# A decoder layer on one core: the DMAs that ScalarE issues are issued by GpSimd instead

## The chip, the cores and the metric

One Trainium2 chip, one of its cores. The metric is the device time of one execution in microseconds (us), as the median of the runs; lower is better. The engines are TensorE (PE; PEld is its weight load), VectorE (DVE), ScalarE (ACT), GpSimd (POOL) and SyncE (SP). SP, ACT and POOL issue DMAs in this kernel. A row that ends in q (ACTq) is an engine's sequencer, which issues or waits while the engine itself is idle.

## The reference, cut to what matters

```python
def reference(x, ...):                       # x: (1, 256, 2048), everything float32
    x = layer_norm(alpha * x + 0.5 * swiglu(x, ffn1...), ln1_g, ln1_b)      # d_ff 5632
    p = x @ w_in                             # 3072 attention columns, 3360 RWKV columns
    o_attn = diff_attn_group(p[..., :3072], ...)    # 8 heads, two softmaxes each, causal, ALiBi
    o_rwkv = rwkv7_group(p[..., 3072:], ...)        # 16 heads of 64, a recurrence over 256 steps
    mix = concatenate([o_attn, o_rwkv]) @ w_out
    x = layer_norm(alpha * x + mix, ln2_g, ln2_b)
    return layer_norm(alpha * x + 0.5 * swiglu(x, ffn2...), ln3_g, ln3_b)
```

The recurrence keeps a 64x64 state per head and updates it at every step by a decay, a rank-one correction and a rank-one addition.

## The kernel before, in words

Three stages follow one another: a feed-forward (FFN), the mixer, a second feed-forward. All large products go through one `Stream`: each weight tile (256 rows by 512 columns, `raw`) is loaded by SP (L125), split into a rounded part `wh` by ACT (L128) and a remainder `wl` by DVE (L129), and used by 12 matmuls (L105 to L107: two halves of the tokens, two row blocks, three products). Seven buffers of `wh` and `wl` let the split run ahead of the matmuls. "A stream step" below is one such tile, and "a stream matmul" one of its 12.

In the mixer the stream carries `w_in` and then `w_out`, and generators (`rwkv_group`, `rwkv_values`, `attn_heads`) put small pieces of background work between the steps. The RWKV heads come in two groups, r1 and r2, and the attention heads in two groups, a1 and a2; a group of attention runs two heads at a time, so a2 has a first and a second pass. `rwkv_group` replaces the recurrence by chunks: it computes products of the chunk's vectors into `Q` (L554 and L557), and needs the inverse of many 32x32 triangular matrices. For that inverse four DMAs rearrange pieces of `Q` into DRAM (`dU`, L566), one brings them back as `U` (L569), DVE runs 31 pairs of instructions (L577 and L579), copies the transposed result (L582), and two DMAs write `dY` and `dYT` (L583, L584), from which four fill `TT` (L591) and two fill `YT` (L595). The four `dU` and the four `TT` DMAs and the two of `YT` move runs of 32 numbers, 512 runs each. Then come products with `YT` (L602), `TT` (L613), transposes (L623), and four chunk steps c0 to c3 (L636, L644, L652, L669, L675), a norm over the heads (L689 to L709) and the gate (L720 to L724).

The output product is taken in three parts, and each part adds to `y`: first a1 and r1, then a2, and last r2.

```python
        for i, qs in enumerate(parts):       # parts = [(0, 2), (1,), (3,)]
            for q in qs:
                ready(q)                     # waits for the group's result and splits it (L78, L79)
            ...
            for n in range(4):
                stream.block(A["w_out"][0], n * NB, NB, ks, o_lhs, ...)
```

Part two needs a2 and has 8 stream steps, 96 matmuls; part three needs r2. Residual pieces `rc` are loaded at L252 (FFN) and L863 (mixer), and `x` is stored to `xs` at L190 between stages. GpSimd computes the powers for the norms (L180, L810), clears `TT` (L589), and loads tables and the norms' gains (L198 to L308).

The tile framework orders every engine's instructions when the program is built, by its own estimate of when each could start. On the chip every engine then takes its instructions in that fixed order. So a change of the issuing engine can reorder all the engines.

Of the kernel before, what the change touches and what calls it, by code (L numbers as in the profile page):

```python
# [20 lines left out]
NB = 512  # L21
# [16 lines left out]
def build(tc, A, out):  # L38
    nc = tc.nc
# [12 lines left out]
    def nm(s):  # L52
        uid[0] += 1
        return f"{s}_{uid[0]}"
# [8 lines left out]
    xs = [dp.tile([P, D], F32, tag=f"xs{t}", name=f"xs{t}") for t in range(2)]  # L63
# [5 lines left out]
    def transpose_split(src, tt, q, store, on_dve=False):  # L69
        tr = tr_bank[-1]()  # L70
        for j in range(4):
            T.transpose(tr[:, j, :], src[:, j * P:(j + 1) * P], ident)
        split(tr, store, tt, q, on_dve)
# [100 lines left out]
    def ln_tail(tt, y, st, gt, bt, last):  # L174
        mv = sp.tile([P, 2], F32, tag="mv", name=nm("mv"))
        V.bn_aggr(out=mv, in_=st)
        ve = sp.tile([P, 1], F32, tag="ve", name=nm("ve"))
        V.tensor_scalar(out=ve, in0=mv[:, 1:2], scalar1=LN_EPS, scalar2=None, op0=ALU.add)
        rs = sp.tile([P, 1], F32, tag="rs", name=nm("rs"))
        G.tensor_tensor(out=rs, in0=ve, in1=neghalf, op=ALU.pow)  # L180
        for q in range(4):
            c = slice(q * NB, (q + 1) * NB)
            yq = y[q]
            V.scalar_tensor_tensor(out=yq, in0=yq, scalar=mv[:, 0:1], in1=gt[:, c], op0=ALU.subtract, op1=ALU.mult)  # L184
            V.scalar_tensor_tensor(out=yq, in0=yq, scalar=rs, in1=bt[:, c], op0=ALU.mult, op1=ALU.add)  # L185
            if last:
                nc.sync.dma_start(out=out[tt * P:(tt + 1) * P, c], in_=yq)
            else:
                transpose_split(yq, tt, q, xT)
                nc.scalar.dma_start(out=xs[tt][:, c], in_=yq)  # L190

    def load_gb(pool, g, b, tg, tb, after=None):
        gt = (hp if tg == "J0" else pool).tile([P, D], F32, tag=tg, name=nm("lng"))
# [8 lines left out]
    def ffn(fp, wg, wu, wd, lg, lb, res, last, extra=None):  # L202
        y = [fp.tile([P, D], F32, tag=f"y{t}", name=nm("y")) for t in range(2)]
        st = [sp.tile([P, 4, 6], F32, tag=f"st{t}", name=nm("st"), bufs=1) for t in range(2)]
        gb = []
        j0 = 0
        for half, nj in enumerate((6, 5)):
            hT = {}
            sg = {}

            def gate_done(tt, acc):
                s = fp.tile([P, NB], F32, tag="sg", name=nm("sg"), bufs=2)
                SC.activation(out=s, in_=acc, func=AF.Silu)  # L213
                sg[tt] = s

            def up_done(tt, acc, j):
                h = fp.tile([P, NB], F32, tag="h", name=nm("h"), bufs=2)
                V.scalar_tensor_tensor(out=h, in0=sg[tt], scalar=0.5, in1=acc, op0=ALU.mult, op1=ALU.mult)  # L218
                tr = tr_bank[-1]()
                for i in range(4):  # L220
                    T.transpose(tr[:, i, :], h[:, i * P:(i + 1) * P], ident)  # L221
                if j < 3:
                    if tt == 0:
                        hT[j] = hp.tile([P, 4, 4, P], F32R, tag=f"J{j}", name=nm("hh"))
                    hi, lo = hT[j][:, 2 * tt], hT[j][:, 2 * tt + 1]
                else:
                    hl = hp.tile([P, 2, 4, P], F32R, tag=f"H{3 * tt + j - 3}", name=nm("hh"))
                    hi, lo = hl[:, 0], hl[:, 1]
                SC.copy(out=hi, in_=tr)  # L229
                V.tensor_tensor(out=lo, in0=tr, in1=hi.bitcast(F32), op=ALU.subtract)  # L230
                hT[(tt, j)] = (hi, lo)

            for j in range(nj):
                c0 = (j0 + j) * NB
                stream.block(wg, c0, NB, KX, x_lhs, gate_done)
                stream.block(wu, c0, NB, KX, x_lhs, lambda tt, acc, j=j: up_done(tt, acc, j))

            def h_lhs(tt, k, hT=hT):
                hi, lo = hT[(tt, k // 4)]
                return hi[:, k % 4, :], lo[:, k % 4, :]  # L240

            if half == 0 and extra is not None:
                extra(hT[(0, 0)][0][:, 0, 0:1].bitcast(F32))
            if half == 1:
                gb = load_gb(fp, lg, lb, "lng", "lnb", hT[(0, 0)][0][:, 0, 0:1].bitcast(F32))

            def down_done(tt, acc, n, half=half, hT=hT):
                c = slice(n * NB, (n + 1) * NB)
                if half == 0:
                    rc = fp.tile([P, NB], F32, tag="rc", name=nm("rc"), bufs=2)  # L250
                    G.tensor_copy(out=rc[:, 0:1], in_=hT[(0, 0)][0][:, 0, 0:1].bitcast(F32))
                    nc.scalar.dma_start(out=rc, in_=res[tt][:, c])  # L252
                    V.scalar_tensor_tensor(out=y[tt][:, c], in0=rc, scalar=ALPHA, in1=acc, op0=ALU.mult, op1=ALU.add)
                else:
                    V.tensor_tensor(out=y[tt][:, c], in0=y[tt][:, c], in1=acc, op=ALU.add)
                    V.bn_stats(out=st[tt][:, n, :], in_=y[tt][:, c])
                    if n == 3:
                        ln_tail(tt, [y[tt][:, i * NB:(i + 1) * NB] for i in range(4)], st[tt], gb[0], gb[1], last)

            for n in range(4):  # L260
                ks = [(j0 * 4 + k, k) for k in range(nj * 4)]
                stream.block(wd, n * NB, NB, ks, h_lhs, lambda tt, acc, n=n, f=down_done: f(tt, acc, n))
            j0 += nj
# [53 lines left out]
    def mix(mp, pq, C):  # L317
# [66 lines left out]
        res = {}  # L384
# [81 lines left out]
        def rwkv_group(g, st):  # L466
# [1 line left out]
            while prev is not None and "chain" not in prev:  # L468
                yield None
            wa = Qt[:, 0:NB]  # L470
            nc.scalar.dma_start(out=wa[0:64, :], in_=A["rwkv_w2"][0, :, g * NB:(g + 1) * NB])
            nc.scalar.dma_start(out=wa[64:128, :], in_=A["rwkv_a2"][0, :, g * NB:(g + 1) * NB])
            while "tw" not in lora:
                yield None
            lw = t4("lw")
# [84 lines left out]
            dU = dp.tile([64, 32, 32], F32, tag="dU", name=nm("dU"))  # L560
            dY = dp.tile([64, 32, 32], F32, tag="dY", name=nm("dY"))
            dYT = dp.tile([32, 32, 32], F32, tag="dYT", name=nm("dYT"))
            quad = [(d, e, slice(64 * e + 32 * d, 64 * e + 32 * d + 32), slice(32 * d, 32 * d + 32),
                     slice(32 * d + 16 * e, 32 * d + 16 * e + 16)) for d in range(2) for e in range(2)]
            for d, e, rr, cc, uu in quad:
                nc.scalar.dma_start(out=dU[uu].rearrange("u s t -> s u t"),  # L566
                                    in_=Q[rr, :, :, e, cc].rearrange("p a c t -> p (a c) t"))
            U = hp.tile([64, 32, 32], F32, tag=HT["T1"], name=nm("U"))
            nc.scalar.dma_start(out=U, in_=dU)  # L569
            Y = hp.tile([64, 32, 32], F32, tag=HT["T2"], name=nm("Y"))  # L570
            V.memset(Y, 0.0)
            V.memset(Y.rearrange("p a b -> p (a b)")[:, ::33], 1.0)
# [7 lines left out]
                if j % 2 == 0:  # L580
                    yield 1.0
            V.tensor_copy(out=U, in_=Y.rearrange("p a b -> p b a"))  # L582
            nc.scalar.dma_start(out=dY, in_=Y)  # L583
            nc.scalar.dma_start(out=dYT, in_=U[0:32])  # L584
            while "values" not in st:
                yield None
            SV = st["SV"]
            TT = hp.tile([P, 16, 64], F32, tag=HT["lw"], name=nm("TT"))
            G.memset(TT, 0.0)  # L589
            for d, e, rr, cc, uu in quad:  # L590
                nc.scalar.dma_start(out=TT[rr, :, cc], in_=dY[uu].rearrange("u s t -> s u t"))  # L591
            YT = hp.tile([P, 16, 32], F32, tag=HT["T1"], name=nm("YT"))
            PT = hp.tile([P, 16, 32], F32, tag=HT["T2"], name=nm("PT"))
            for e in range(2):
                nc.scalar.dma_start(out=YT[64 * e:64 * e + 32], in_=dYT[16 * e:16 * e + 16].rearrange("u s t -> s u t"))  # L595
            yield 0.6
            Qf = Q.rearrange("p a c e t -> p (a c) e t")
            ps = bank("sm", (P, 16, 32))
# [81 lines left out]

            st["chain"] = True
            g2a, g2b = Qt[:, 3072:3584], Qt[0:32, 3584:4096]
            nc.scalar.dma_start(out=g2a, in_=A["rwkv_g2"][0, 0:128, g * NB:(g + 1) * NB])
            nc.scalar.dma_start(out=g2b, in_=A["rwkv_g2"][0, 128:160, g * NB:(g + 1) * NB])
            for hf in range(2):
                h2 = slice(2 * hf, 2 * hf + 2)
                ps = bank("sm", (P, 2, S))
# [171 lines left out]
        def o_done(tt, acc, n, i):  # L859
            c = slice(n * NB, (n + 1) * NB)  # L860
            if i == 0:
                rc = mp.tile([P, NB], F32, tag="tm", name=nm("rc"), bufs=2)
                nc.scalar.dma_start(out=rc, in_=xs[tt][:, c])  # L863
                V.scalar_tensor_tensor(out=y[tt][n], in0=rc, scalar=ALPHA, in1=acc, op0=ALU.mult, op1=ALU.add)
            else:
                V.tensor_tensor(out=y[tt][n], in0=y[tt][n], in1=acc, op=ALU.add)  # L866
            if i == len(parts) - 1:
                V.bn_stats(out=st[tt][:, n, :], in_=y[tt][n])  # L868
                if n == 3:
                    ln_tail(tt, y[tt], st[tt], gb[0], gb[1], False)  # L870
# [79 lines left out]
```

## Time and profile before

| | |
|---|---|
| median of 3 runs | 2022.41 us (2021.51 to 2024.14) |
| the profiled execution: its time, its span | 2021.85 us, 2020.1 us |
| PE busy | 1976.9 us, 98% of the span, 9671 matmuls |
| DVE, ACT, POOL busy | 1149.0, 887.6, 33.9 us |
| DMA queue q10 (issued by ACT) | 17440 packets, 14.29 MB |
| DMA queue q0 (issued by POOL) | 1520 packets, 6.93 MB |
| granted TensorE clock | 0.989 of full speed on average |

PE is busy nearly all the time, so the page as a whole says little about what an off-path DMA is worth. The stretch that tells more is the mixer's end, from about 1148 us to 1234 us of the span: there the granted clock falls and PE waits.

### The profile page before, as it was taken

To read this page: it belongs to the slowest core of one execution; us is meant where nothing else is said; L and a number is where in the kernel's file an instruction comes from. 1 tells how busy PE (TensorE), PEld (TensorE's weight loads), DVE (VectorE), ACT (ScalarE), POOL (GpSimd) and SP (SyncE) were. 2 spreads that over 40 slices of the span, in tenths; PEclk is the share of its full clock that TensorE was granted. 3 is DMA by queue.
4 is the path that set the end of the run, shared out by engine and by line. 5 is a ranking of instruction groups with operands and counts; after the bars stand their busy time and mean duration, and the time that the engine had idled before them with its cause. 6 is when DMAs were issued, how large, how long until landed. Compare 5 with 4: busy or idle time off the path is not lost. (4 is left out here: it accounts for less than half of the span.)

```text
span 2020.1 us, 24928 instructions
## 1 busy us (share of the span) xinstructions
PE 1976.9 (98%) x9671; PEld 1614.6 (80%) x9671; DVE 1149.0 (57%) x1420; ACT 887.6 (44%) x1100; POOL 33.9 (2%) x68
## 2 busy tenths in 40 slices
PE   9999999999999999999999988999999999999997
PEld 7888888888888878888777777788888888888886
DVE  5555544445554566776677866755554444555455
ACT  5444433344444337645574444444443334444432
POOL 0200000000000000000000000000000000000000
PEclk9999999999999999999999979999999999999999
DMA  7766666667666556556435624666666666766553
GB/s 248 214 188 195 186 190 202 205 192 229 193 187 189 188 171 194 177 160 178 139 86 177 198 84 148 210 198 188 196 185 190 203 204 191 230 193 187 189 188 125
DMA packets 202008, 373.35 MB, mean 185 GB/s; under 512 B 22826, under 2 KB 24944, under 8 KB 201120
## 3 DMA queue, kind: packets, MB, share of 16 engines
q1 hardware_dynamic: 182928, 350.53, 58.0%
q10 hardware_dynamic: 17440, 14.29, 2.4%
q0 software_dynamic: 1520, 6.93, 1.0%
q8 instruction: 76, 1.25, 0.3%
q14 instruction: 44, 0.36, 0.1%
HBM read 364.10 MB, written 7.60 MB: 184 GB/s over the span
## 5 line engine op out<-in xcount | busy, mean ns | idle before, releaser
L129 DVE TENSOR_TENSOR wl<-raw,wh 128x1024 fp32r<-128x1024 f32 (+1 forms) x665 | 808.2, 1216 | 662.4 <-ACT wh L128 661.3
L128 ACT CAST wh<-raw 128x1024 fp32r<-128x1024 f32 (+1 forms) x665 | 695.2, 1046 | 851.9 <-PE acc L107 736.8
L107 PE MATMUL acc<-wh,xl 128*128 128x512 f32 (+1 forms) x1952 | 740.7, 391 | 1.6 <-DVE xl L79 1.6
L106 PE MATMUL acc<-wl,xh 128*128 128x512 f32 (+1 forms) x1952 | 736.7, 392 | 1.0 <-DVE wl L129 1.0
L105 PE MATMUL acc<-wh,xh 128*128 128x512 f32 (+1 forms) x1952 | 725.5, 392 | 9.0 <-ACT xh L78 7.6
L105 PEld LDWEIGHTS acc<-wh,xh 128*128 128x128 f32 x1952 | 367.9, 189 | 88.7 <-ACT xh L78 9.3
L106 PEld LDWEIGHTS acc<-wl,xh 128*128 128x128 f32 x1952 | 368.1, 189 | 77.5 <-issue 2.0
L107 PEld LDWEIGHTS acc<-wh,xl 128*128 128x128 f32 x1952 | 367.8, 188 | 76.3 <-DVE xl L79 2.0
L107 PE MATMUL acc<-wh,hh 128*128 128x512 f32 x704 | 258.0, 395 | 0.0
L106 PE MATMUL acc<-wl,hh 128*128 128x512 f32 x704 | 256.7, 394 | 0.0
L105 PE MATMUL acc<-wh,hh 128*128 128x512 f32 x704 | 256.0, 394 | 0.0
L106 PEld LDWEIGHTS acc<-wl,hh 128*128 128x128 f32 x704 | 132.0, 187 | 31.4
L107 PEld LDWEIGHTS acc<-wh,hh 128*128 128x128 f32 x704 | 132.0, 188 | 31.2
L105 PEld LDWEIGHTS acc<-wh,hh 128*128 128x128 f32 x704 | 132.0, 188 | 30.9
L230 DVE TENSOR_TENSOR hh<-tr,hh 128x512 fp32r<-128x512 f32 x44 | 30.4, 691 | 64.4 <-ACT hh L229 64.4
L229 ACT CAST hh<-tr 128x512 fp32r<-128x512 f32 x44 | 25.8, 586 | 91.7 <-PE tr L221 91.6
L218 DVE SCALAR_TENSOR_TENSOR h<-sg,acc 128x512 f32<-128x512 f32 x44 | 30.3, 688 | 35.6 <-PE acc L107 35.6
L213 ACT ACTIVATE sg<-acc 128x512 f32<-128x512 f32 x44 | 26.4, 600 | 43.8 <-PE acc L107 43.7
L577 DVE TENSOR_TENSOR itmp<-U,Y 64x31 f32<-64x31 f32 (+15 forms) x62 | 20.6, 332 | 11.5 <-DMA U<-dU 10.2
L221 PEld LDWEIGHTS tr<-ident,h 128*128 128x128 f32 x176 | 21.8, 139 | 5.7
L221 PE MATMUL tr<-ident,h 128*128 128x128 f32 x176 | 26.3, 272 | 0.0
L579 DVE TENSOR_TENSOR Y<-Y,itmp 64x31 f32<-64x31 f32 (+15 forms) x62 | 20.6, 332 | 1.4
(247 smaller groups left out, 750.2 us busy)
## 6 DMA issues: line engine op xcount, KB each, us to landing
raw<-in_ffn_w_up_dram SPq DMA_DIRECT2D x176, 512.0 KB, 3.9
raw<-in_ffn_w_down_dram SPq DMA_DIRECT2D x176, 512.0 KB, 4.1
raw<-in_ffn_w_gate_dram SPq DMA_DIRECT2D x175, 512.0 KB, 3.9
raw<-in_w_in_dram SPq DMA_DIRECT2D x96, 512.0 KB, 3.9
raw<-in_w_out_dram SPq DMA_DIRECT2D x32, 512.0 KB, 4.6
rc<-xs ACTq DMA_DIRECT2D x16, 256.0 KB, 4.0
lng<-in_ln_g_dram POOLq DMA_DIRECT2D x3, 1024.0 KB, 7.0
lnb<-in_ln_b_dram POOLq DMA_DIRECT2D x3, 1024.0 KB, 9.3
```

The lines of the kernel that those rows point to most:

```text
L105: T.matmul(a, hi, wh[:, j, :w], start=(ki + j == 0), stop=False)
L106: T.matmul(a, hi, wl[:, j, :w], start=False, stop=False)
L107: T.matmul(a, lo, wh[:, j, :w], start=False, stop=(ki + j == last))
L128: SC.copy(out=wh[:, c, :w], in_=raw[:, c, :w])
L129: V.tensor_tensor(out=wl[:, c, :w], in0=raw[:, c, :w], in1=wh[:, c, :w].bitcast(F32), op=ALU.subtract)
L213: SC.activation(out=s, in_=acc, func=AF.Silu)
L218: V.scalar_tensor_tensor(out=h, in0=sg[tt], scalar=0.5, in1=acc, op0=ALU.mult, op1=ALU.mult)
L221: T.transpose(tr[:, i, :], h[:, i * P:(i + 1) * P], ident)
L229: SC.copy(out=hi, in_=tr)
L230: V.tensor_tensor(out=lo, in0=tr, in1=hi.bitcast(F32), op=ALU.subtract)
L577: V.tensor_tensor(out=tv, in0=U[:, 0:j, j:j + 1].to_broadcast([64, j, 32 - j]), in1=Y[:, j:j + 1, j:32].to_broadcast([64, j, 32 - j]), op= ...
L579: V.tensor_tensor(out=Y[:, 0:j, j:32], in0=Y[:, 0:j, j:32], in1=tv, op=ALU.add)
```

## The change

Every `nc.scalar.dma_start` becomes `nc.gpsimd.dma_start`, at 15 places in the text; shapes, tiles and data stay.

```diff
@@ ln_tail
-                nc.scalar.dma_start(out=xs[tt][:, c], in_=yq)
+                nc.gpsimd.dma_start(out=xs[tt][:, c], in_=yq)
@@ ffn, down_done
-                    nc.scalar.dma_start(out=rc, in_=res[tt][:, c])
+                    nc.gpsimd.dma_start(out=rc, in_=res[tt][:, c])
@@ rwkv_group
-            nc.scalar.dma_start(out=wa[0:64, :], in_=A["rwkv_w2"][0, :, g * NB:(g + 1) * NB])
-            nc.scalar.dma_start(out=wa[64:128, :], in_=A["rwkv_a2"][0, :, g * NB:(g + 1) * NB])
+            nc.gpsimd.dma_start(out=wa[0:64, :], in_=A["rwkv_w2"][0, :, g * NB:(g + 1) * NB])
+            nc.gpsimd.dma_start(out=wa[64:128, :], in_=A["rwkv_a2"][0, :, g * NB:(g + 1) * NB])
@@
-                nc.scalar.dma_start(out=dU[uu].rearrange("u s t -> s u t"),
+                nc.gpsimd.dma_start(out=dU[uu].rearrange("u s t -> s u t"),
-            nc.scalar.dma_start(out=U, in_=dU)
+            nc.gpsimd.dma_start(out=U, in_=dU)
@@
-            nc.scalar.dma_start(out=dY, in_=Y)
-            nc.scalar.dma_start(out=dYT, in_=U[0:32])
+            nc.gpsimd.dma_start(out=dY, in_=Y)
+            nc.gpsimd.dma_start(out=dYT, in_=U[0:32])
@@
-                nc.scalar.dma_start(out=TT[rr, :, cc], in_=dY[uu].rearrange("u s t -> s u t"))
+                nc.gpsimd.dma_start(out=TT[rr, :, cc], in_=dY[uu].rearrange("u s t -> s u t"))
@@
-                nc.scalar.dma_start(out=YT[64 * e:64 * e + 32], in_=dYT[16 * e:16 * e + 16].rearrange("u s t -> s u t"))
+                nc.gpsimd.dma_start(out=YT[64 * e:64 * e + 32], in_=dYT[16 * e:16 * e + 16].rearrange("u s t -> s u t"))
@@
-            nc.scalar.dma_start(out=g2a, in_=A["rwkv_g2"][0, 0:128, g * NB:(g + 1) * NB])
-            nc.scalar.dma_start(out=g2b, in_=A["rwkv_g2"][0, 128:160, g * NB:(g + 1) * NB])
+            nc.gpsimd.dma_start(out=g2a, in_=A["rwkv_g2"][0, 0:128, g * NB:(g + 1) * NB])
+            nc.gpsimd.dma_start(out=g2b, in_=A["rwkv_g2"][0, 128:160, g * NB:(g + 1) * NB])
@@ mix, o_done
-                nc.scalar.dma_start(out=rc, in_=xs[tt][:, c])
+                nc.gpsimd.dma_start(out=rc, in_=xs[tt][:, c])
```

How the built order moves is shown at three places, all near the end of the mixer. `Y` is the inverse being built for r2, `ars` and `ot` belong to a2's heads, `wl` to the stream.

POOL, from the clearing of r2's `TT` on. Before:

```order
L589 MEMSET TT_8541 128x1024
L810 TENSOR_TENSOR ars_9282<-vr_9280,neghalf 128x4
L810 TENSOR_TENSOR ars_9296<-vr_9294,neghalf 128x4
L810 TENSOR_TENSOR ars_9500<-vr_9498,neghalf 128x4
L810 TENSOR_TENSOR ars_9532<-vr_9530,neghalf 128x4
```

POOL at the same place, now, from the second power on:

```order
L810 TENSOR_TENSOR ars_9296<-vr_9294,neghalf 128x4
L583 DMA dY_8150<-Y_8158 64x1024
L584 DMA dYT_8151<-U_8156 32x1024
L591 DMA TT_8541<-dY_8150 32x16x32 x4
L595 DMA YT_8547<-dYT_8151 32x16x32 x2
L863 DMA rc_9685<-xs_83 128x512
L863 DMA rc_9773<-xs_83 128x512
L810 TENSOR_TENSOR ars_9500<-vr_9498,neghalf 128x4
```

The DMAs of the inverse's result now stand behind the two powers of a2's first pass, and two residual loads stand behind them, ahead of the powers of the second pass.

DVE, from the stream's tile `wl_9648` to the end of r2's inverse. Before, the inverse has five instructions to go after that tile:

```order
L129 TENSOR_TENSOR wl_9648<-raw_9646,wh_9647 128x1024
L579 TENSOR_TENSOR Y_8158<-Y_8158,itmp_8511 64x3x29
L577 TENSOR_TENSOR itmp_8514<-U_8156,Y_8158 64x60
L579 TENSOR_TENSOR Y_8158<-Y_8158,itmp_8514 64x2x30
L577 TENSOR_TENSOR itmp_8535<-U_8156,Y_8158 64x31
L579 TENSOR_TENSOR Y_8158<-Y_8158,itmp_8535 64x31
L582 COPY U_8156<-Y_8158 64x1024
```

Now, from the same tile on (the first rows of the stretch):

```order
L129 TENSOR_TENSOR wl_9648<-raw_9646,wh_9647 128x1024
L577 TENSOR_TENSOR itmp_8449<-U_8156,Y_8158 64x231
L579 TENSOR_TENSOR Y_8158<-Y_8158,itmp_8449 64x11x21
L577 TENSOR_TENSOR itmp_8452<-U_8156,Y_8158 64x220
L579 TENSOR_TENSOR Y_8158<-Y_8158,itmp_8452 64x10x22
L129 TENSOR_TENSOR wl_9666<-raw_9664,wh_9665 128x1024
L577 TENSOR_TENSOR itmp_8455<-U_8156,Y_8158 64x207
L129 TENSOR_TENSOR wl_9698<-raw_9696,wh_9697 128x1024
L579 TENSOR_TENSOR Y_8158<-Y_8158,itmp_8455 64x9x23
L804 TENSOR_SCALAR ot_9278<-at_9274 128x256
```

Between `wl_9648` and the copy L582 there now stand 22 instructions of the inverse (11 pairs), 4 stream tiles, and the whole norm of a2's first pass: for each of its two heads L804, L809, L812, L808, L811, L813, L814, L815 and two of L817, and for the first head L822.

PE, where the products with `YT` begin. Before they follow on the stream's last matmul that does not need a2:

```order
L107 MATMUL acc_9621<-wh_9585,xl_9148 128x512
L602 MATMUL sm_8551<-YT_8547,Q 32x32 x32
L613 MATMUL sm_8588<-TT_8541,PT_8548 32x32
L623 MATMUL sm_8643<-ident,BKc 128x64 x8
L821 MATMUL at_9342<-ident,ot_9278 128x128 x2
```

Now:

```order
L107 MATMUL acc_9621<-wh_9585,xl_9148 128x512
L821 MATMUL at_9342<-ident,ot_9278 128x128 x2
L821 MATMUL at_9364<-ident,ot_9292 128x128 x2
L766 MATMUL at_9372<-k_8086,qq 128x128
L766 MATMUL at_9372<-k_8086,qq 128x256
L766 MATMUL at_9373<-k_8086,qq 128x128
L766 MATMUL at_9373<-k_8086,qq 128x256
L766 MATMUL at_9402<-k_8086,qq 128x128
L766 MATMUL at_9402<-k_8086,qq 128x256
L766 MATMUL at_9403<-k_8086,qq 128x128
L766 MATMUL at_9403<-k_8086,qq 128x256
L787 MATMUL at_9460<-ident,s_9368 128x128
```

Right behind the last row stands L602. The end of a2's first pass, the scores of its second pass and the first transpose of their softmax (L787) have moved ahead of L602. Further on, the 96 stream matmuls of part two, which stood behind the L636 of chunk step c3, now stand between c0 and c3: 15 between c0 and the L636 of c1, 57 from there to c2's and 24 from there to c3's. Behind c3's L636 there are none.

## Rows read from the trace of the kernel before

**Rows 1.** The page's part 1: busy us (share) xinstructions of each engine.

```profile
PE 1976.9 (98%) x9671; PEld 1614.6 (80%) x9671; DVE 1149.0 (57%) x1420; ACT 887.6 (44%) x1100; POOL 33.9 (2%) x68
```

**Rows 2.** Windows: start:end, us, busy of PE, PEld, DVE, ACT, POOL, PEclk, DMA.

```profile
1148.00:1196.00 48.00, 37.65 (x482) 30.21 (x481) 31.41 (x96) 22.02 (x71) 4.03 (x4) 0.75 0.34 100
1196.00:1234.00 38.00, 32.10 (x177) 25.38 (x178) 22.45 (x29) 16.21 (x19) 1.14 (x2) 0.96 0.45 146
```

**Rows 3.** Waits, 1080 to 1240 us: us in total, times, longest.

```profile
PE acc L105 <- ACT xh L78: 6.7, 2, 5.9
...
ACT ot L806 <- DMA TT<-dY: 5.7, 1, 5.7
DVE itmp L577 <- DMA U<-dU: 5.0, 1, 5.0
```

**Rows 4.** PE's timeline, 1156 to 1236 us: start, us, engine, line, operation.

```profile
1157.80 1.54 PE L602 MATMUL sm<-YT,Q 32*32 32x32 f32 x64 [1.71 <-DMA YT<-dYT]
...
1169.87 1.12 PE L636 MATMUL sm<-SV,Q 64*64 64x64 f32 x16
...
1180.21 0.90 PE L787 MATMUL at<-ident,s 128*128 128x128 f32 x3
...
1188.23 0.69 PE L636 MATMUL sm<-SV,Q 128*64 128x64 f32 x16
...
1194.07 0.97 PE L636 MATMUL sm<-SV,Q 128*64 128x64 f32 x16
1195.86 0.50 PE L105 MATMUL acc<-wh,xh 128*128 128x512 f32 x1 [0.82 <-ACT xh L78]
...
1212.82 1.89 PE L689 MATMUL sm<-BKc,bones 128*128 128x256 f32 x8
...
1233.70 0.79 PE L105 MATMUL acc<-wh,xh 128*128 128x512 f32 x1 [5.90 <-ACT xh L78]
```

**Rows 5.** DVE's timeline at the end of r2's inverse, and two rows of a2's heads.

```profile
1124.79 0.39 DVE L577 TENSOR_TENSOR itmp<-U,Y 64x231 f32<-64x231 f32 x1
...
1145.70 1.23 DVE L129 TENSOR_TENSOR wl<-raw,wh 128x1024 fp32r<-128x1024 f32 x1 [0.19 <-ACT wh L128]
...
1147.83 0.18 DVE L579 TENSOR_TENSOR Y<-Y,itmp 64x31 f32<-64x31 f32 x1
1148.04 1.14 DVE L582 COPY U<-Y 64x1024 f32<-64x1024 f32 x1
...
1165.22 0.61 DVE L817 TENSOR_SCALAR ot<-at,ars 128x128 f32<-128x128 f32 x2
...
1169.97 0.56 DVE L768 SCALAR_TENSOR_TENSOR s<-dist,at 128x384 f32<-128x384 f32 x1 [1.09 <-PE at L766]
```

**Rows 6.** ACT's timeline, 1148 to 1157 us.

```profile
1148.04 0.49 ACTq L583 DMA_DIRECT2D dY<-Y  x1
...
1153.30 1.95 ACTq L591 DMA_DIRECT2D TT<-dY  x4
1155.34 0.98 ACTq L595 DMA_DIRECT2D YT<-dYT  x2
1156.37 0.31 ACT L806 ACTIVATE ot<-ot 128x128 f32<-128x128 f32 x1 [5.72 <-DMA TT<-dY]
```

**Rows 7.** The chain of work that ended last, 1140 to 1240 us: start, us, what.

```profile
1222.33 1.28 ACT L700
```

**Rows 8.** POOL's timeline: DMAs of 8 and of 128 rows, and L180.

```profile
60.47 0.50 POOL L278 DMA_DIRECT2D vr<-in_rwkv_k_k_dram  x1
...
66.57 0.54 POOL L305 DMA_DIRECT2D smask<-in_smask_dram  x1
...
754.05 0.99 POOL L180 TENSOR_TENSOR rs<-ve,neghalf 128x1 f32<-128x1 f32 x1 [12.19 <-DVE ve L178]
```

**Rows 9.** DMA issues: names, issuer, count, KB each, median us to landing.

```profile
rc<-xs ACTq DMA_DIRECT2D x16, 256.0 KB, 4.0
...
smask<-in_smask_dram POOLq DMA_DIRECT2D x1, 128.0 KB, 4.6
```

## The prediction, made before the run

> **What bounds the kernel now.** I read the page's first part, then the busy time by windows, then who waited for whom in the mixer, and last the timelines of PE, DVE, ACT and POOL around the place where PE runs dry. The page says that PE is busy 98% of the span [rows 1], so nothing off PE's path is worth anything, and at most some 43 us can be won at all. The windows show where that path leaves PE: from 1148 to 1196 us PE is busy for 37.65 of 48 us at a mean granted clock of 0.75, and from 1196 to 1234 for 32.10 of 38 [rows 2]. There the path is the second RWKV group, r2: its inverse, the rearranging DMAs, the products with `YT`, four chunk steps, the norm and the gate. PE's waits name it [rows 3]: stream matmuls wait 6.7 us for the split of a result (ACT L78), 5.90 of them before the matmul at 1233.70, where part three of the output product finds r2 finished [rows 4].
>
> The times that the sum uses: r2's inverse ends with the copy at 1148.04 [rows 5], `YT` is there when L602 starts at 1157.80, c0's L636 starts at 1169.87, c3's at 1194.07, the stream resumes with part two at 1195.86 and with part three at 1233.70 [rows 4]. Before 1148 us PE has stream work to hide things under. After 1234 us everything hangs on PE again, so a delay of r2's end is a delay of the kernel's end, one for one, as long as part two's 96 matmuls are used up first.
>
> **What is off the path.** The FFN's residual loads and the stores to `xs` move to POOL, which is busy for 33.9 us in all [rows 1]. A load is asked for one buffer ahead and takes 4.0 us to land [rows 9]; ACT loses about half a microsecond per issue and was 44% busy [rows 1]. I take 0 for both. Cover: the stream. Were it gone, each load would cost its 4 us. At the norms the power L180 now queues behind four stores; the second one in LN1 runs at 754.05, after 12.19 us in which POOL had nothing to do [rows 8], so four issues of about 0.54 us fit. The small mixer weights are loaded long before their use: 0. Group r1 is rearranged under stream matmuls: 0 here, with its upper end in the range.
>
> **The inverse of r2 ends later: +14.7.** The order now puts the norm of a2's first pass, more stream tiles and most of the inverse behind `wl_9648`. Before, that tile started at 1145.70 and took 1.23, so it ended at 1146.93 [rows 5]. PE paces the stream's tiles, so I let it stand at the same time. Then come 22 instructions of the inverse, from 0.39 down to 0.18 us [rows 5], 0.29 each on average: 6.3. Four tiles of 1.23: 4.9. Four of L817, two of which take 0.61: 1.2; and 17 small ones that I estimate at 0.2 each from the smallest row of the same engine (0.18): 3.4. The copy then starts at 1146.93 + 15.8 = 1162.7, against 1148.04. The bounds: 3, if DVE's waits (5.0 us for `U` alone [rows 3]) take up most of the added work, and 20, if POOL's powers keep DVE waiting. I take the sum, since DVE has hardly a gap in those rows.
>
> **The rearranging itself: +1.1.** ACT began the four `TT` DMAs in 1.95 us and the two of `YT` in 0.98, after `dY` in 0.49 [rows 6]. POOL's own issues take 0.50 us for 8 rows and 0.54 for 128 [rows 8]. No row of POOL has 512 runs. If only the slope between these two counts, 512 runs take 0.67 us and six of them 4.0 against 2.93: +1.1. If all of the 0.54 grows with the runs, one takes 2.16 and six take 13.0: +10. Less than nothing is excluded by the 0.50. I take the lower value, since the rows of 8 and 128 lie so close. The landing I leave as it is: 4.6 us for POOL's 128 KB beside 4.0 for ACT's 256 KB [rows 9] shows no sure difference. The same holds for the four `dU`: 0 to +6.7 (8.6 against 1.95), and I take 0, because the order puts more tiles ahead of the first L577, which waited 5.0 us for `U` before [rows 3].
>
> The Trainium skill, "DMA: Bandwidth & Descriptors", section "Specifications", speaks against the change: it gives about 1 us to the first byte for DMAs that GpSimd issues and about 0.6 for those of SP and ACT. Four transfers stand in series in r2 (`dU`, `U`, `dY`, `TT` or `YT`), so by that page the sum would be some 1.6 us higher, which is an estimate from its figures; the rows named above show neither for nor against.
>
> **What is queued behind it: +1.5.** L602 now stands behind L787, the first transpose of a2's second pass. That pass can start when the copy (1.14 us) and one more L822 (some 0.5) are through, at 1164.3; from its first L768 to L787 it took 10.2 us, 1169.97 to 1180.21 [rows 4, 5]. So L602 starts at 1174.6, while `YT` would be there at 1157.80 + 14.7 + 1.1 = 1173.6: +1.0. On DVE the copy of L602's result stands behind a residual sum whose load POOL issues only after `YT`: 0.54 to issue and 4.0 to land [rows 8, 9], against 1.5 for `YT` to land and 1.54 for L602: 0.5 more.
>
> **The rest of r2 gets shorter: -7.8.** Before, from c0's L636 to the end took 63.8 us (1169.87 to 1233.70), the first 24.2 of it without stream matmuls. Now a2 is through earlier, and all 96 stand between c0 and c3. They are 0.23 us apart, 22 us, and three chunk steps have about 3.5 us of PE work each, so c0 to c3 takes about 33 (bounds 24.2 and 46). From c3 on nothing covers the latencies: the last 11.4 us from L700 on [rows 7] stay, and c3 up to there has 6.9 us of PE instructions (L689 and its like take 1.89 [rows 4]) and five hand-overs of about 1 us: 23 in all (at least 17.6, which is 39.6 less the 22). 33 + 23 is 56, and 7.8 less than 63.8.
>
> **The clock: +2.** In the stretch that was without stream matmuls the mean granted clock is 0.75, in the one with them 0.96 [rows 2], a mix of 2.4 and 1.2 GHz. The tail from c3 on is now such a stretch, and its two norm products take 3.8 us at full clock; between 0 and 3.8 more I take 2.
>
> **The sum.** 14.7 + 1.1 + 1.5 - 7.8 + 2 = +11.5 us. The profiled execution took 2021.85 us: its span of 2020.1 and 1.75 around it. 2021.85 + 11.5 = 2033.4, and the median of the runs stands 0.56 above the profiled one, so 2034.
>
> **The rivals.**
>
> First, POOL's cost grows with the number of runs. For it speaks that no row of POOL has anything but plain rows; against it the flat 0.50 to 0.54 [rows 8]. Then +10 at `TT` and `YT`, +6.7 at `dU`, less about 2 that L787 would have cost anyway: 2034 + 15 = 2049, and up to 2058 if r1's PE has to wait too.
>
> Second, faster: ACT no longer stands for 5.72 us in front of the `TT` DMAs, during which a2's L806 was ready [rows 6]. If DVE's idle time takes up the new work, so that the copy L582 starts before 1151, the first term is under 3.2 and the sum turns negative; with that term at 0 and the tail at its least, 17.6, the sum is -8.6: 2014. Against it: DVE is dense there.
>
> Third, no change: the later inverse and the shorter rest cancel. By the Trainium skill, the same page, section "Issuing engines are not separate DMA queues", the issuing engine only saves sequencer time; that alone would leave the kernel where it is. As a mechanism of this kernel: ACT's issues are no part of the path, the copy comes some 3 to 7 us later, 2018.4 to 2026.5. Against it: the order of DVE's rows, which is fixed.
>
> **How the numbers follow.** The forecast (2027 to 2042) has 0.52, the first rival 0.25, the second 0.12, the third 0.11. A measurement of this kernel can tell about 0.2% from no change, 4 us here. So faster is 0.12, the same 0.11, slower 0.77. The range of 2014 to 2054 takes in the second rival's price and most of the first's; the slower cases alone span 2027 to 2058.
>
> **What would show it.** Right: in r2 the copy L582 near 1163, the `TT` and `YT` issues of POOL at 0.6 to 0.7 us each, L602 near 1175 with L787 just ahead, stream matmuls between c0 and c3, and about 23 us from c3's L636 to part three without any, ending near 1245. Wrong: `TT` issues of 2 us and more, or PE waiting for `YT` in r1 (the first rival); the copy before 1151 (the second); part three starting where it did (the third). A wait of PE outside the mixer would make the whole reading wrong.

## The result and the profile after

The changed kernel takes 2027.28 us, median of 11 runs (2023.70 to 2029.85); the kernel before takes 2022.41 in 11 runs beside it (2021.26 to 2025.61). The ratio is 1.002, 95% interval 1.001 to 1.0029: slower by 4.9 us, where 11.5 were forecast. The range held the time, at its lower edge; the size did not hold.

The profiled execution of the changed kernel took 2023.76 us, one of its quickest. So both programs were traced again, unchanged (see the experiments), and the account below uses three traces of before and four of after. The page's part 1 and its row of POOL's DMA queue, after (compare [rows 1]):

```profile
PE 1976.9 (98%) x9671; PEld 1615.6 (80%) x9671; DVE 1150.2 (57%) x1420; ACT 888.8 (44%) x1100; POOL 78.2 (4%) x142
q0 software_dynamic: 6192, 21.22, 3.4%
```

POOL is busy 44.3 us more, and no other engine less: 74 issues more count as its busy time. Windows of the changed kernel, columns as in [rows 2]; the second ends with r2's result:

```profile
1148.00:1196.00 48.00, 38.33 (x350) 30.44 (x350) 31.23 (x95) 20.39 (x59) 10.86 (x14) 0.68 0.23 72
1196.00:1238.00 42.00, 31.06 (x284) 23.61 (x283) 22.81 (x36) 14.27 (x19) 2.21 (x4) 0.95 0.37 123
```

In the first, PE's clock is lower than before (0.68 for 0.75) with 132 fewer matmuls done. DVE's timeline (start, us, then the instruction). r2's first pair in the kernel before:

```profile
1093.31 0.20 DVE L577 TENSOR_TENSOR itmp<-U,Y 64x31 f32<-64x31 f32 x1 [4.97 <-DMA U<-dU]
```

In the changed kernel: r2's first pair, tile `wl_9648`, the copy.

```profile
1098.63 0.19 DVE L577 TENSOR_TENSOR itmp<-U,Y 64x31 f32<-64x31 f32 x1
...
1139.97 1.22 DVE L129 TENSOR_TENSOR wl<-raw,wh 128x1024 fp32r<-128x1024 f32 x1 [0.72 <-ACT wh L128]
...
1156.02 1.03 DVE L582 COPY U<-Y 64x1024 f32<-64x1024 f32 x1
```

The tile that I had left where it was ends at 1141.19, 5.7 us earlier than in [rows 5]. The copy comes 14.8 us after it, near the 15.8 that I had added up, but at 1156.02 and not at 1162.7. Over all traces of both kernels that tile ends 4.1 us earlier on average, and r2's first pair starts 6.9 us later (1098.6 to 1100.7 against 1092.1 to 1093.3): 371 of the stream's tiles stand ahead of it on DVE, 366 before. POOL's timeline behind the tile:

```profile
1155.87 1.30 POOL L583 DMA_DIRECT2D dY<-Y  x1 [0.80 <-DVE ot L817]
1157.35 0.50 POOL L584 DMA_DIRECT2D dYT<-U  x1 [0.18 <-issue]
1160.09 2.63 POOL L591 DMA_DIRECT2D TT<-dY  x4 [2.23 <-DMA dY<-Y]
1162.70 0.65 POOL L595 DMA_DIRECT2D YT<-dYT  x1
1164.00 0.66 POOL L595 DMA_DIRECT2D YT<-dYT  x1 [0.64 <-issue]
```

One issue of 512 runs takes 0.65 to 0.69 us (the row of four averages 0.66); 0.67 was the estimate, 2.16 the first rival's. The rest of r2 on PE's timeline:

```profile
1164.76 0.45 PE L787 MATMUL at<-ident,s 128*128 128x128 f32 x1 [3.32 <-DVE s L782]
1165.29 0.31 PE L602 MATMUL sm<-YT,Q 32*32 32x32 f32 x2
...
1166.58 1.91 PE L602 MATMUL sm<-YT,Q 32*32 32x32 f32 x62 [0.36 <-DMA YT<-dYT]
...
1178.42 1.12 PE L636 MATMUL sm<-SV,Q 64*64 64x64 f32 x16
...
1216.73 1.04 PE L636 MATMUL sm<-SV,Q 128*64 128x64 f32 x16
...
1221.65 1.99 PE L689 MATMUL sm<-BKc,bones 128*128 128x256 f32 x8 [0.47 <-ACT BKc L676]
...
1237.82 0.79 PE L105 MATMUL acc<-wh,xh 128*128 128x512 f32 x1 [6.21 <-ACT xh L78]
```

PE does wait for L787 in front of L602, but that wait cost nothing to speak of: the first half of `YT`, issued at 1162.70, lands 2.5 us later, when L787 is through as well. Part two lies between c0 (1178.42) and c3 (1216.73), and part three starts at 1237.82 against 1233.70 [rows 4].

All traces together, in us. "r2's end" is the start of ACT's L78, 0.67 before part three; the last row goes on to the 411th weight split in the second FFN, behind LN2, from where on the traces run in parallel:

| step | before, 3 traces | after, 4 traces | difference of the means | forecast |
|---|---|---|---|---|
| r2's copy L582 starts | 1146.6 to 1148.0 | 1156.0 to 1158.8 | +10.0 | +14.7 |
| copy to L602 | 9.6 to 10.3 | 9.1 to 9.3 | -0.8 | +2.1 |
| L602 to c0's L636 | 11.8 to 12.1 | 13.1 to 13.2 | +1.3 | +0.5 |
| c0 to r2's end | 63.0 to 63.9 | 58.2 to 61.0 | -4.3 | -5.8 |
| together: r2's end | 1231.8 to 1233.1 | 1237.2 to 1239.9 | +6.3 | +11.5 |
| r2's end to the split behind LN2 | 54.1 to 56.0 | 53.4 to 54.8 | -1.3 | 0 |

The sum is +5.0 us, close to the 4.9 by which the medians differ. One shift inside the table is only one of marks: in the changed kernel two of L602's 64 matmuls start with the first half of `YT`, and the other 62 start 10.4 to 10.6 us behind the copy. Counted to these the second step is 0.6 us longer, and the third, at 11.8, as long as before. The traces enter the mixer up to 4.6 us apart. Where that matters, times below are counted from the start of the stream's 273rd tile on DVE, called the tile at 762 us (760.2 to 764.8 in all traces).

### The profile page after: what moved, and what is told of

It is laid out like the page before. It is cut to its first block, busy times and chain, and to the rows that moved or that the text cites. A ratio compares the mean times of both kernels' runs of the same rounds, so it can differ in the third digit from the quotient of the medians.

```text
span 2021.9 us, 24991 instructions
## 1 busy us (share of the span) xinstructions
PE 1976.9 (98%) x9671; PEld 1615.6 (80%) x9671; DVE 1150.2 (57%) x1420; ACT 888.8 (44%) x1100; POOL 78.2 (4%) x142
## 4 chain that ended last, share of the span: by engine, by line
PE 88%; DVE 6%; DMA 2%; ACT 2%; issue 1%; POOL 0%; SPq 0%; DVEq 0%; ACTq 0%; POOLq 0%
PE acc L105 28%; PE acc L106 28%; PE acc L107 27%; DVE wl L129 2%; PE tr L221 1%; DMA raw<-in_ffn_w_gate_dram 1%; ACT wh L128 1%; DMA raw<-in_w_out_dram 0%; PE sm L554 0%; DMA raw<-in_ffn_w_up_dram 0%; DVE y L184 0%; PE tr L342 0%; DVE y L185 0%; PE sm L636 0%; DVE itmp L577 0%
## 5 line engine op out<-in xcount | busy, mean ns | idle before, releaser
L180 POOL TENSOR_TENSOR rs<-ve,neghalf 128x1 f32<-128x1 f32 x6 | 6.1, 1013 | 609.1 <-DVE ve L178 609.1
```

## The experiments

**The transfers without the inverse's.** Residual pieces, copies of x and small weights go to GpSimd, the thirteen DMAs of each rearranging stay on ScalarE (the change without L566 to L595).

```diff
-            nc.scalar.dma_start(out=rc, in_=xs[tt][:, c])
+            nc.gpsimd.dma_start(out=rc, in_=xs[tt][:, c])
...
```

> Everything but the inverse's rearranging is issued by GpSimd (residual pieces, copies of x, small weights); the rearranging stays on ScalarE. One stream tile more than before stands ahead of r2's copy, no norm. Theory (order of DVE's work): copy at 1148 to 1150, 2021 to 2025 us. Rival (residual loads behind other DMAs of GpSimd, or the powers of the norms behind the stores, cost what the change cost): 2026 us or more, with waits of DVE for rc at L253 or L864 or a later L180 in the profile.

2025.28 against 2024.20 us, ratio 1.0002 (0.9994 to 1.0011); copy at 1149.29, r2's end at 1235.85. These moves cost nothing that can be told from zero, so the change's loss needs the rearranging. One thing more is in this trace: ScalarE issued `YT`, and it landed late all the same, with SP beginning three weight loads between 1152 and 1162 us.

```profile
YT<-dYT ACTq DMA_DIRECT2D x2, 64.0 KB, 5.7
```

L602 began 12.1 us behind the copy.

**r2's result alone.** dY, dYT, TT and YT of r2 are issued by GpSimd; up to r2's copy all engines keep the order of before.

```diff
-            nc.scalar.dma_start(out=dY, in_=Y)
+            (nc.gpsimd if g == 1 else nc.scalar).dma_start(out=dY, in_=Y)
...
```

> Only r2's result (dY, dYT, TT, YT) is issued by GpSimd; all else stays on ScalarE. Up to r2's copy L582 the order of all engines is that of the kernel before. Theory (the order of DVE's work costs, the issuer does not): the copy stays at 1148.0, L602 starts within 1.5 us of 1157.8, ScalarE no longer waits 5.7 us before TT, a2's first pass comes earlier, and the rest from c0 to r2's end shortens by up to the 4.4 us seen in the changed kernel: 2017 to 2021 us. Rival (GpSimd's issues are what costs, by a later YT or a slower landing): L602 2 us or more later, 2024 us or more.

2030.30 us, 1.003 (1.0019 to 1.0041): slower than the whole change. The copy stood at 1150.14, but L602 began 15.9 us behind it. My theory had no such wait. SyncE's timeline from 1152 to 1164 us and the trace's DMA issues (count, KB each, median us to landing) of this kernel:

```profile
1152.42 8.73 SPq L125 DMA_DIRECT2D raw<-in_w_out_dram  x4
```
```profile
YT<-dYT POOLq DMA_DIRECT2D x2, 64.0 KB, 7.2
```

YT took 7.2 us, and in these twelve microseconds SP began four weight loads of 512 KB. In the same twelve microseconds of the changed kernel there is one, 6.3 us ahead of TT, and YT lands in 2.5:

```profile
1153.74 0.37 SPq L125 DMA_DIRECT2D raw<-in_w_out_dram  x1
```

In the kernel before, YT landed in 2.3 to 2.8 us in the three traces (medians of its two DMAs), and SP began no load between 1150.4 and 1158.1. Is it GpSimd's queue, or the collision? The next run takes the loads away and leaves the queue.

**The same with the loads held.** A tiny store of YT on SP's queue makes SP wait for it ahead of the later weight loads.

```diff
+            if g == 1: stream.hold = nc.sync.dma_start(out=dp.tile([1, 8], F32, tag="dH", name=nm("dH")), in_=YT[64:65, 0, 0:8]).ins
...
+                    with tc.issue_after(self.hold) if 1846 <= uid[0] - 2 < 1900 else ExitStack(): nc.sync.dma_start(out=raw[:, c, :w], ...)
```

> Only r2's result is issued by GpSimd, as in the run of 2030.3 us, and SP waits for YT to land before it begins the weight loads from the fourth tile behind r2's copy on (a tiny store of YT on SP's queue in front of them). Theory (the 512 KB weight loads that fly at the same time make YT land in 7.2 us instead of 2.4): YT lands in 2.3 to 3.5 us, L602 starts 10 to 12 us after the copy instead of 15.9, and the time is 2023 to 2027. Rival (GpSimd's queue itself is slow when it issues the result): the landing stays above 6 us and the time at 2030.

2024.86 us against 2023.69, 1.0004 (0.9995 to 1.0013). SP's timeline over the same twelve microseconds, and the DMA issues:

```profile
1158.27 0.31 SPq L596 DMA_DIRECT2D dH<-YT  x1
1158.67 1.41 SPq L125 DMA_DIRECT2D raw<-in_w_out_dram  x3
```
```profile
YT<-dYT POOLq DMA_DIRECT2D x2, 64.0 KB, 2.5
```

With the loads behind it YT lands in 2.5 us, and some 5 us of the kernel are back. So the issuer of r2's result costs about nothing, though its issues are longer; what costs is which loads the transfers meet, and the 5.7 us above show it with ScalarE as issuer. The Trainium skill, "DMA: Bandwidth & Descriptors", section "Issuing engines are not separate DMA queues", says that transfers of all issuers interleave on the same DMA engines; 7.2 against 2.5 agrees.

**The norm pinned behind the copy.** In the changed kernel, a2's first norm may start on DVE only after r2's L582.

```diff
-            V.tensor_copy(out=U, in_=Y.rearrange("p a b -> p b a"))
+            st["copy"] = V.tensor_copy(out=U, in_=Y.rearrange("p a b -> p b a")).ins
...
+                with tc.issue_after(r2["copy"]) if g == 1 and h < 2 else ExitStack(): V.tensor_scalar(out=ot, ...)
```

> The changed kernel, with the norm of a2's first pass pinned behind r2's copy L582 on DVE; 21 of the 25 instructions that newly stood ahead of the copy are behind it again, four stream tiles (4.9 us) stay ahead. Theory (the copy is late by the work that stands ahead of it on a full DVE, 9.3 us by its records): the copy comes 4.4 us earlier than in the changed kernel, at 1151 to 1153 instead of 1156.0, and L602 follows it 9 to 10 us later. Rival (the copy is late because U lands late: the first L577 was at 1098.6 instead of 1093.3): the copy stays at 1155 to 1156. The time of the kernel: 2020 to 2025 by the theory, 2027 or more by the rival.

Copy at 1155.40, 0.6 us earlier than in the first trace of the changed kernel and not 4.4; 2028.15 us, 1.002 (1.0011 to 1.0029): the rival's numbers. The 0.6 is too little, since r2's first pair starts 1.3 us later in this trace (1099.97). Windows from the first pair to the copy, the changed kernel and then this one:

```profile
1098.63:1156.02 57.39, 52.12 (x248) 41.70 (x246) 51.66 (x130) 26.77 (x55) 6.52 (x10) 1.00 0.58 189
1099.97:1155.40 55.43, 51.66 (x245) 41.44 (x243) 49.29 (x111) 25.48 (x47) 4.23 (x7) 1.00 0.60 190
```

The stretch became 2.0 us shorter, and 2.0 to 2.9 against the four traces. DVE is busy for 2.4 us less, not for 4.4: its small instructions overlap in the trace, so their summed durations say too much. Its idle time in the stretch is about the same (6.1 us for 5.7). So work ahead counts here by the time that it keeps DVE busy, and not by its durations. The tiles that are left wait in part for ACT, as its timeline shows:

```profile
1142.88 1.05 ACT L128 CAST wh<-raw 128x1024 fp32r<-128x1024 f32 x1 [1.36 <-DMA raw<-in_w_out_dram]
1145.80 1.05 ACT L128 CAST wh<-raw 128x1024 fp32r<-128x1024 f32 x1 [1.87 <-DMA raw<-in_w_out_dram]
```

The copy still stands behind four more tiles than before the change.

**The four tiles pinned too.**

```diff
+                    with tc.issue_after(self.copy) if 1824 < uid[0] < 1860 else ExitStack(): V.tensor_tensor(out=wl[:, c, :w], ...)
```

> The changed kernel with the norm of a2's first pass and the next four stream tiles pinned behind r2's copy L582 on DVE: ahead of the copy stand as many tiles (384) and norms as in the kernel before, and GpSimd issues everything. In the run that pinned the norm alone the copy came only 0.6 us earlier than in the changed kernel, since the four tiles arrive at the pace of their loads. Theory (the tiles ahead of the copy make it late): the copy comes 6 to 8 us earlier, at 1148 to 1150. What it is worth: if only the copy counts, the time is 2019 to 2022; if the loads of the stream, which are then still under way, slow the landing of YT (7.2 us in the run with r2's result alone on GpSimd, 2.4 before and after), L602 starts 12 us or more after the copy instead of 9.3, and the time stays at 2024 to 2029.

Copy at 1150.61, 5.4 us earlier than in the first trace of the changed kernel. Yet 2030.04 us, 1.0034 (1.0022 to 1.0047): the transfers now meet the loads again.

```profile
1153.50 6.79 SPq L125 DMA_DIRECT2D raw<-in_w_out_dram  x4
```
```profile
YT<-dYT POOLq DMA_DIRECT2D x2, 64.0 KB, 6.3
```

**Tiles pinned and loads held:** both edits, and the hold begins with the fourth tile behind the copy.

```diff
+                    with tc.issue_after(self.hold) if 1842 <= uid[0] - 2 < 1900 else ExitStack(): nc.sync.dma_start(out=raw[:, c, :w], ...)
```

> The changed kernel with the norm and the four tiles pinned behind r2's copy (the run of 2030 us), and besides the weight loads from the fourth tile behind the copy on held until YT has landed. Theory (with the copy early, what is left of the loss is the collision of YT with the weight loads): YT lands in 2.3 to 3.5 us instead of 6.3, L602 starts 9 to 11 us after the copy instead of 13.7, and the time is 2024 to 2027. Rival (the loss of 6 us of that run lies elsewhere, in the order of the chunk steps): 2029 or more in spite of an early L602.

YT lands in 2.4 us and L602 comes 9.1 us after the copy instead of 13.7, as expected. The time was missed: 2029.32 us, 1.0027 (1.0016 to 1.0038). From the copy to r2's end it takes 86.5 us against 90.1 without the hold, but 81.1 in the changed kernel: the rival has that part. The kernel before, where part two also lies around c3, takes 85.0 to 85.3, so this run has lost the shorter rest and little more. What it keeps is a late copy: counted from the tile at 762 us, r2's first pair starts at 338.0 us as in the changed kernel (337.8 to 338.2; before 329.7 to 331.7), and the copy stands at 390.3 (before 384.5 to 386.4). The pins could not reach the late start.

**r1's rearranging alone on GpSimd, and all but r1's.** At L566 to L595, in the kernel before and in the changed one:

```diff
+            (nc.gpsimd if g == 0 else nc.scalar).dma_start(...)
```
```diff
+            (nc.gpsimd if g == 1 else nc.scalar).dma_start(...)
```

> GpSimd issues the rearranging of r1 alone, ScalarE all else. Theory (the first L577 of r2 comes 5 to 7 us later in the changed kernel because r1's rearranging on GpSimd reorders the first group): first L577 of r2 at 1097 to 1101 instead of 1093.3, the copy of r2, with 386 tiles ahead of it, at 1151 to 1155, and 2024 to 2029 us. Rival (the reordering comes from r2's own dU and result): first L577 within 2 us of 1093.3 and 2021 to 2024.

2024.20 us, 1.0007 (0.9999 to 1.0016); first L577 at 1096.70, copy at 1153.01: between theory and rival.

> The changed kernel with r1's rearranging back on ScalarE; GpSimd issues all else. 387 stream tiles and one of the two norms of a2's first pass stand ahead of r2's copy (388 and both in the changed kernel, 384 and none before). Theory (the late start of r2's inverse in the changed kernel comes from r1's rearranging on GpSimd, the rest of the lateness from the tiles and norms ahead of the copy): first L577 of r2 within 2 us of 1093 instead of 1098.6 to 1100.7, the copy at 1151 to 1155, YT landing in 2.3 to 3 us since the loads have stopped by then, and 2023 to 2027 us. Rival (the start is late through r2's own DMAs or the small loads): first L577 at 1097 or later and 2026 to 2030.

2023.87 against 2022.28 us, 1.0009 (1.0 to 1.0018). DVE's timeline:

```profile
1093.47 0.19 DVE L577 TENSOR_TENSOR itmp<-U,Y 64x31 f32<-64x31 f32 x1
...
1152.76 1.01 DVE L582 COPY U<-Y 64x1024 f32<-64x1024 f32 x1
```

As expected, the first pair is near 1093 us again. With r1 alone on GpSimd it was this:

```profile
1096.70 0.20 DVE L577 TENSOR_TENSOR itmp<-U,Y 64x31 f32<-64x31 f32 x1 [2.32 <-DMA U<-dU]
```

In the changed kernel r1's L602 stands some three stream steps later on PE and starts at 933.7 instead of 927.0; r2's inverse then starts at 1098.6 to 1100.7 instead of 1092.1 to 1093.3. Counted from the tile at 762 us the first pair comes at 329.7 to 331.7 us before, at 337.8 to 338.2 in the changed kernel, at 333.5 with r1 alone and at 332.8 with all but r1. So r1's moves alone bring 3.0 of the 7.5 us, and 5.2 go when they are taken back; the rest needs the other moves too, and which of them was not tried. Of the copy's 10.0 us, 6.9 are the late first pair and 3.1 a longer way from it to the copy, where the norm stands.

**A late copy with ScalarE as issuer.** Seven passes over Y ahead of r2's copy in the kernel before.

```diff
+            for j in range(7 * g): V.tensor_scalar(out=Y, in0=Y, scalar1=1.0, scalar2=None, op0=ALU.mult)
             V.tensor_copy(out=U, in_=Y.rearrange("p a b -> p b a"))
```

> The kernel before (ScalarE issues all its DMAs) with seven passes over Y (64 x 1024, multiplied by 1.0) put in front of r2's copy L582 on DVE, so that the copy comes late as in the changed kernel; three more stream tiles then stand ahead of it, and part two's matmuls lie between c0 and c3 as there. Theory (order and lateness of r2's inverse cost the change its time, not the issuer): copy at 1155 to 1159, r2's end 3 to 8 us later than in the kernel before, 2025 to 2030 us. Rival (GpSimd as the issuer costs): with ScalarE as issuer the later copy is absorbed by the shorter rest, 2020 to 2024.

Copy at 1161.13 (the passes took more than I gave them), 2030.16 us, 1.0032 (1.002 to 1.0044). A late copy costs with ScalarE too: 6.5 us for a copy 11.7 us later, counted from the tile at 762 us, where the changed kernel pays 4.9 for 10.6.

**r2's tail ahead of part two**, in the kernel before: part two's stream matmuls may start on PE only after r2's L689.

```diff
...
+                    stream.tail = T.matmul(ps[:, p, :], C["bones"], Yc[:, 2 * hf + p], start=True, stop=True).ins
...
+                with tc.issue_after(self.tail) if getattr(self, "tail", None) is not None and blk.get("pin") else ExitStack(): T.matmul(a, hi, wh[:, j, :w], ...)
```

> The kernel before (ScalarE issues) with the stream matmuls of part two pinned behind the L689 of r2's norm on PE, so that chunk step c3 and the norm no longer queue behind them. Theory (the 39.6 us from c3 to part three are long since c3's instructions stand between part two's matmuls; in the changed kernel, where these are used up, the same piece took 20.6): c3 to L700 takes about 10 us instead of 28, r2's end comes near 1216, part two ends near 1226 and part three follows at once: 2014 to 2019 us. Rival (the piece is long for its own latencies, or L700 waits behind the casts L128): part three not before 1231, 2020 to 2025.

c3 to L700 fell from 28.3 to 16.0 us (10 were expected) and r2's end came at 1226.25. The time stayed: 2023.80 against 2023.69, 1.0005 (0.9995 to 1.0015). The theory fell at its end; windows of this kernel, the second one LN2, and LN2 in the kernel before:

```profile
1188.00:1260.00 72.00, 67.36 (x437) 54.62 (x435) 47.96 (x83) 29.92 (x49) 3.15 (x4) 0.93 0.43 137
1260.00:1278.00 18.00, 10.14 (x43) 8.17 (x42) 17.75 (x29) 6.53 (x8) 1.56 (x2) 0.72 0.71 213
...
1260.00:1278.00 18.00, 14.52 (x58) 11.38 (x57) 17.96 (x27) 5.30 (x8) 1.00 (x1) 0.81 0.72 216
```

PE is idle for 7.9 of the 18 us in LN2 (3.5 in the same window of the kernel before), with DVE busy for 17.75 of them. A part of what was won at r2's end is lost there. The other part was no gain: from the tile at 762 us to r2's end PE is idle for 16.4 us here and for 16.0 to 18.6 before, so the earlier end mostly put part two's matmuls behind it.

**Loads held in the kernel before** (the hold, from the fourth tile on), for a version that beats both.

> The kernel before (ScalarE issues all its DMAs), with the weight loads from the fourth tile behind r2's copy on held until YT has landed. Theory (collisions with weight loads are what lengthens r2's transfers): dY lands in 3.3 to 4.3 us instead of 5.2, YT in 2.3 as before, L602 starts 8 to 9.5 us after the copy instead of 9.8, and the time is 2020 to 2024, at best 2 us below the kernel before. Rival (holding loads back starves the stream later): PE waits for tiles between 1165 and 1230, 2025 or more.

2022.93 against 2023.42 us, 1.0002 (0.9993 to 1.0011): the same. YT lands in 2.5 us, as it did without, and L602 starts 9.9 us behind the copy, so nothing of the expected 8 to 9.5 came. No version here beats the kernel before.

**The two kernels traced again.**

> The changed kernel once more, unchanged. Its runs lay between 2023.7 and 2029.85 us; the profiled one was 2023.76 with a mean granted clock of 0.988, most others showed 0.986. Theory: the runs differ in the clock alone. In the profile shown, the stretch of LN2 (1266 to 1278 us) has a granted clock of 1.00, where the kernel before had 0.71; a run of 2027 us or more should show a half-clock stretch there or in the mixer's end that the first profile lacks, and r2's copy L582 at 1156.0 within 0.5 us. Rival: the runs differ in the DMAs' landing, so that the copy or the start of L602 moves by 2 us or more at the same clock.

> The kernel before, unchanged, for a second trace. Theory: traces of one program agree within the mixer (from the tile at 762 us to r2's end at 1233: 471.4 us, within 1 us) and differ in the two norms LN1 and LN2 by the granted clock; the first trace of the kernel before has half clock at 1268 to 1274 in LN2. Rival: the mixer itself varies by 3 us or more from run to run, and the single traces of the experiments say little.

> The changed kernel, unchanged, for a third trace. Theory: in the mixer it is 4.9 to 5.5 us longer than the kernel before (476.4 and 476.9 us from the tile at 761 us to r2's end in its two traces); what lies between its quick runs (2023.7) and most of them (2027 to 2029.9) is LN1 and a half-clock stretch in LN2, some 30 us behind r2's end, that its two traces do not have: with it 2027 or more and a mean clock of 0.986. Rival: a slow run shows its time in the mixer, as a later YT or a later copy.

A third pair stood beside it. The mixer, from the tile at 762 us to r2's end, took 471.4, 470.5 and 469.7 us before, and 476.4, 476.9, 479.5 and 476.9 after. That is less steady than expected, by up to 3 us. The second trace of the changed kernel had the copy at 1158.80 and not near 1156.0, as its rival had it; 1.9 of these 2.8 us are there at the tile at 762 already. The long one has L689 at half clock (compare 1.99 us above):

```profile
1222.66 3.78 PE L689 MATMUL sm<-BKc,bones 128*128 128x256 f32 x8 [0.47 <-ACT BKc L676]
```

No traced run of the changed kernel took 2027 us or more, so why most of its runs are slower than its quickest stays open. Single traces carry 2 to 3 us of chance, in the mixer's end and in LN1 and LN2, and the verdicts above rest on the medians.

## Why the prediction was wrong, step by step

**Right:** the place (r2, behind 1148 us), the sign, and the mechanism: a later inverse, partly paid back by a shorter rest, with nothing for the FFN's loads and stores. Right too the issue: 0.65 us for 512 runs, so the first rival is out. The second is out, with a copy at 1156 and later. The third gave 2018.4 to 2026.5 and comes close; what it said of the issuer proved true for r2's result, the equal time did not, and the copy came 10.0 us later, not 3 to 7.

**The step that failed: "PE paces the stream's tiles, so I let it stand at the same time."** `wl_9648` ended 5.7 us earlier in the first trace, 4.1 on average. Of the 22 instructions of the inverse that I counted behind it, 17 had stood ahead of it before (the built order shows 5 behind it), and these take 5.5 us. On an engine that is nearly full, moving work behind an instruction moved the instruction forward. From the tile's end to the copy it then took 15.3 us on average, near the 15.8 of the sum. So the term measured +10.0 and not +14.7, and the tile is where the difference lies. To count what is new ahead of the copy, four tiles and the norm, 25 instructions of 9.3 us by their durations, would have come near by luck. With all of them pinned away the copy, counted from the tile at 762 us, came only 5.6 us earlier. And two terms that the sum had put at 0 hid the late first pair of 6.9 us: "0 here" for r1, and 0 for the `dU`, "because the order puts more tiles ahead of the first L577". The five tiles more ahead of it were the order's doing, and they were not priced.

**"The rearranging itself: +1.1" and "+1.5" behind it.** Copy to L602 became 0.8 us shorter, not 2.1 longer (0.6 longer to the 62 that wait for all of `YT`). L787 does stand in front, but the softmax from L768 to L787 took 6.5 us (1158.27 to 1164.76) and not 10.2. The wait of L864 for its residual load was 0.71 us, next to the 0.5 forecast, and almost hidden under L602. And the transfers met fewer loads: dY landed in 3.6 us (4.5 to 5.2 before). "The landing I leave as it is" was the weakest sentence of the sum: in the two runs where GpSimd's `YT` followed a copy at 1150, L602 came 13.7 and 15.9 us behind the copy. YT lands in 2.4 to 2.5 us from GpSimd and 2.3 to 2.8 from ScalarE. So the 1.6 us that the Trainium skill, "DMA: Bandwidth & Descriptors", section "Specifications", would add (an estimate from its first-byte figures) do not show at `YT`. In the quickest landings the page's difference of some 0.4 us does show: the quickest `xs<-y` took 2.4 us from ScalarE and 2.7 to 2.8 from GpSimd, counted from the start of the issue.

**"-7.8" and "the clock: +2".** c0 to the end became 4.3 us shorter, 5.8 forecast: c0 to c3 took 38.3 us in the first trace for the 33 forecast, c3 to the end 20.4 for 23. The clock's term was real in one trace of four, with 2 to 3 us there. Half clock stood elsewhere too: 62 of L602's matmuls took 1.91 us at a granted clock of 0.50, where all 64 took 1.54 before at 0.96.

**"One for one."** From r2's end to the split behind LN2 1.3 us came back, and in the run that ended r2 early nothing of it reached the time. Part two's matmuls then still had to run, and behind them stands the next bound, LN2, where DVE is full.

## What to carry to other kernels

To price a reordering on a full engine, count the instructions that are new ahead of the one that matters; never fix one of the moved neighbours in time. Price them by the time that they keep the engine busy and not by their summed durations, and ask whether the stretch itself starts later. Before giving small, many-run transfers on the critical path a landing time, look at which bulk loads will be under way when they start: making them earlier or later can matter more than which engine issues them. And an earlier end of one stage is worth nothing until the next stage's own bound has been read.

## What the runs showed of the hardware

- Two transfers of 64 KB in 512 runs each landed in 2.3 to 2.8 us with no weight load begun beside them, in 6.3 and 7.2 us with four of 512 KB begun in the same twelve microseconds (GpSimd issuing), and in 5.7 with three (ScalarE issuing).
- A GpSimd issue took 0.49 to 0.53 us for dYT, 0.65 to 0.72 for 512 runs and 0.88 to 1.30 for dY (64 rows into DRAM); ScalarE's for 512 runs and for dY took 0.49 on average [rows 6].
- DVE's instructions overlap in the trace: 21 of the norm with durations of 4.4 us kept it busy for 2.4 us (51.66 with them and 49.29 without, from r2's first pair to the copy).
